# Modulation weights laid out by output, and 24 more gathered rows multiplied during routing

## The chip, the cores and the metric

The kernel runs on one core of one Trainium2 chip. The metric is the device time of one execution in microseconds (us), the median of repeated runs.

## What is computed

The model is a two-layer decoder trunk over 512 tokens of width 1024. Each layer is a mixer (RWKV-7 time mixing beside a pooling mixer) and then an expert feed-forward part (PEER). Both are preceded by RMSNorm and by a modulation: a shift, a scale and a gate for every channel, all computed from one conditioning vector `c`. The reference, cut to what this case touches:

```python
c_act = silu(c)                                   # (1, 1024)
for l in range(2):
    mod = c_act @ ada_w[l] + ada_b[l]             # (1, 6 * 1024)
    sh1, sc1, g1, sh2, sc2, g2 = split(mod, 6)
    h = rmsnorm(x, ln1_g[l]) * (1 + sc1) + sh1
    x = x + g1 * mixer(h)
    h2 = rmsnorm(x, ln2_g[l]) * (1 + sc2) + sh2
    x = x + g2 * peer(h2)

def peer(h):
    q = h @ peer_q                                # 8 heads, 2 halves of 128
    s, i = top_k(q . keys, 16)                    # per token, head and half
    top_s, sel = top_k(s0 + s1, 16)               # 16 of 256 pairs per token and head
    idx, gate = pairs[sel], softmax(top_s)        # 128 experts per token
    act = gelu(h . u[idx])                        # u, v: 16384 rows of 1024
    return sum(gate * act * v[idx])
```

## The kernel before

TensorE (PE) multiplies 128x128 blocks. The weights in fp32 are split into a high and a low part by ScalarE (ACT, line 281) and VectorE (DVE, line 282), and each product takes three matmuls of the parts (`mm3`, line 299). `split_next` loads a weight tile into one of three `raw` buffers and splits it into one of three `wsp` buffers, so the split runs at most three tiles ahead of PE.

The 512 tokens of a layer's PEER part are treated in two ways. For the last 384 tokens ("dense"), all 16384 experts are computed in 128 chunks of 128 experts: `s_chunk` multiplies the tokens with a chunk of `u` (24 matmuls of 384 columns), then gelu, then a multiplication by a gate table, then `back` multiplies with the chunk of `v` (18 matmuls of 512 columns, line 1193). For the first 128 tokens ("gathered"), only the 128 chosen experts per token are read: one indirect DMA on the GpSimd queue (POOL, line 884) fetches one row of `u` or of `v` for each of the 128 tokens, a tile of 128x1024 fp32. There are 128 tiles of `u` and 128 of `v` in each layer. DVE multiplies each `u` tile with the tokens and sums along the row (line 890, with a second instruction that reads the sum), and each `v` tile is added into the output with its weight (line 898).

The stages of a layer, in the order of the program, are these.

1. The mixer, lines 340 to 840. At its start in layer 0 four groups of modulation values are computed (`ada_both`, lines 204 to 220) before the first projection can run; six more groups in each layer's mixer (`ADA_MIX`) are computed beside the mixer's work (`ada_step`, line 782).
2. The query stage, lines 1080 to 1095: 16 query projections, each followed by scores and by four top-16 selections on DVE. Beside it, six more groups of modulation values in layer 0 and two in layer 1 (`ADA_PRE`).
3. Routing. For each of the four token tiles DVE picks the 16 best pairs of each head (`pick`). POOL multiplies the masks (line 1002), DVE sums them (line 988). For the three dense tiles it then builds one-hot tables (lines 1055 to 1058), which PE turns into the gate table (line 1075). The picks of the third and fourth tile run interleaved with the first 32 of 48 one-hot blocks; the last 16 blocks run without picks. Beside all routing, the first `SPILL` = 88 chunks of `u` are multiplied (`s_ahead`) and their gelu is written to memory. In the part with one-hot blocks, the first `GPRE` = 24 gathered tiles are loaded and multiplied (`gather_step`), three buffers at a time.
4. The dense stage, the loop of lines 1237 to 1247: `front`, `values`, `gathers` and `back` for each chunk. Chunks 0 to 87 read their gelu back; chunks 88 to 127 compute it. The function `upto` says how many gathered tiles are loaded by chunk c: 0.9 per chunk up to chunk 87, then the rest evenly until `GEND` = 4 chunks before the end. With 24 + 79 tiles done by chunk 87, 153 are left for 36 chunks, 4.25 for each.
5. The ends: the last three chunks are multiplied tile by tile, and `finish` and `update` treat each token tile, the gathered one (number 0) first.

Each modulation group is 512 outputs. Its weights lie by input: a tile holds 128 inputs x 512 outputs. DVE multiplies eight such half tiles with a per-partition scalar and adds them up (line 195 for the first, line 197 for the other seven). Four matmuls with a column of ones (line 227) then sum over the partitions. Each of these is two weight loads and two passes on PE, eight in all for a group. At the start of layer 0, `ada_both` gives half of the eight tiles directly to PE (line 213). Each engine runs its instructions in a fixed order; a scheduler sets it when the program is built, from the order of the code, the buffers, and its own estimate of when things are ready.

## Time and profile before

| what | value |
|---|---|
| median of 3 runs | 3393.1 us (3392.6 to 3399.39) |
| profiled execution: its own time | 3396.74 us |
| profiled execution: span of the trace | 3395.0 us |
| PE busy (weight loads beside it) | 3211.9 us, 95% (2810.6 us, 83%) |
| DVE busy | 2713.8 us, 80% |
| ACT, POOL busy | 1397.3 us, 41%; 828.7 us, 24% |
| mean granted PE clock | 0.957 of full speed |
| moved by DMA | 826.48 MB, mean 243 GB/s |

The span runs from the first to the last instruction; the 1.7 us between it and the execution's own time lie around the trace. Busy shares are means over stages with different limits, so each stage is read by itself, in windows of time.

### The profile page before, as it was taken

The numbers are of one execution on the slowest core, as the hardware profiler recorded it, in microseconds if no ns is written. First come the engines' busy times: TensorE is split into PE (matmuls) and PEld (weight loads), VectorE is DVE, ScalarE is ACT, GpSimd is POOL, SyncE is SP. The second block draws the span as 40 slices with busy tenths as digits, with TensorE's granted clock in tenths as the row PEclk, the third lists the DMA queues.
The fourth block names the chain that finished last, engine by engine and source line by source line (L and its number), as shares of the span: only waits on it lengthen the run. The fifth ranks groups of instructions, "written<-read, shape, count | busy, mean of one in ns | idle before, by whom it ended". The sixth has DMA issues, their size and how long they took to land. (4 is left out here: it accounts for less than half of the span.)

```text
span 3395.0 us, 52138 instructions
## 1 busy us (share of the span) xinstructions
PE 3211.9 (95%) x18762; PEld 2810.6 (83%) x18762; DVE 2713.8 (80%) x6065; ACT 1397.3 (41%) x2281; POOL 828.7 (24%) x675
## 2 busy tenths in 40 slices
PE   7999889999999999999999999999999999999997
PEld 5787678989998888888777877899999788888886
DVE  4577599888868888899938766988887688888888
ACT  2543223455653334333353523334556433333333
POOL 0000001232202222655500000032230222255554
PEclk8988899999999999999999989999999999999998
DMA  5224353577799999999922234256778999999996
GB/s 192 69 69 151 109 164 118 175 238 255 258 324 346 343 347 337 353 396 383 361 79 86 83 106 155 77 161 195 261 250 291 329 341 340 341 351 335 356 353 260
DMA packets 361380, 826.48 MB, mean 243 GB/s; under 512 B 46496, under 2 KB 189600, under 8 KB 357792
## 3 DMA queue, kind: packets, MB, share of 16 engines
q1 hardware_dynamic: 287392, 554.68, 48.7%
q0 software_dynamic: 73728, 268.47, 21.0%
q8 instruction: 147, 2.41, 0.3%
q14 instruction: 113, 0.93, 0.1%
HBM read 730.75 MB, written 92.27 MB: 242 GB/s over the span
## 5 line engine op out<-in xcount | busy, mean ns | idle before, releaser
L1193 PE MATMUL ps<-vv,wg 128*128 128x512 f32 x4608 | 1081.0, 393 | 23.0 <-ACT vv L1176 11.9
L299 PE MATMUL pss<-hi,wsp 128*128 128x384 f32 (+1 forms) x4880 | 1002.2, 356 | 66.4 <-DVE wsp L282 28.2
L1193 PEld LDWEIGHTS ps<-vv,wg 128*128 128x128 f32 x4608 | 869.1, 189 | 209.1 <-ACT vv L1176 17.5
L299 PEld LDWEIGHTS pss<-hi,wsp 128*128 128x128 f32 x4880 | 879.2, 193 | 126.5 <-DVE wsp L282 38.3
L281 ACT ACTIVATE wsp<-raw 128x1024 fp32r<-128x1024 f32 x341 | 359.6, 1056 | 517.4 <-PE pss L299 352.3
L884 POOL DMA_INDIRECT row<-u,ex x256 | 319.6, 1249 | 845.7 <-DVE row L890 649.6
L299 PE MATMUL pss<-lo,wsp 128*128 128x384 f32 (+1 forms) x2440 | 501.6, 346 | 0.0
L282 DVE TENSOR_TENSOR wsp<-raw,wsp 128x1024 fp32r<-128x1024 f32 x341 | 426.0, 1250 | 66.8 <-ACT wsp L281 65.4
L299 PEld LDWEIGHTS pss<-lo,wsp 128*128 128x128 f32 x2440 | 436.5, 189 | 17.4 <-issue 0.8
L884 POOL DMA_INDIRECT row<-v,ex x256 | 336.8, 1316 | 244.3 <-DVE ox L898 196.1
L1177 DVE TENSOR_TENSOR vv<-raw,vv 128x512 fp32r<-128x512 f32 x512 | 344.4, 690 | 41.7 <-ACT vv L1176 41.6
L1176 ACT ACTIVATE vv<-raw 128x512 fp32r<-128x512 f32 x512 | 291.2, 618 | 110.6 <-DMA raw<-v 74.8
L1167 ACT ACTIVATE wg<-ge 128x384 fp32r<-128x384 f32 x256 | 133.0, 524 | 492.3 <-DVE ge L1165 198.3
L890 DVE SCALAR_TENSOR_TENSOR row<-row,hx 128x1024 f32<-128x1024 f32 x256 | 310.8, 1219 | 24.5 <-DMA row<-u,ex 24.4
L898 DVE SCALAR_TENSOR_TENSOR ox<-row,wx,ox 128x1024 f32<-128x1024 f32 x254 | 325.3, 1281 | 2.3
L1002 POOL TENSOR_TENSOR eq<-same,cid 128x400 f32<-128x400 f16 x128 | 146.8, 1167 | 502.3 <-DVE same L998 307.2
L966 POOL TENSOR_TENSOR hf<-hi,lo 128x128 f32<-128x128 f32 x16 | 8.1, 524 | 933.8 <-DVE tw L935 877.6
L1168 DVE TENSOR_TENSOR wg<-ge,wg 128x384 fp32r<-128x384 f32 x256 | 141.4, 555 | 104.4 <-ACT wg L1167 99.8
L1077 ACT ACTIVATE gb<-ps 128x512 f32<-128x512 f32 x192 | 200.1, 1163 | 0.0
L1165 DVE TENSOR_TENSOR ge<-ge,g 128x192 f32<-128x192 f32 x496 | 157.0, 353 | 49.9 <-DMA g<-gscr 32.2
L1160 ACT ACTIVATE ge<-pss 128x384 f32<-128x384 f32 x80 | 39.2, 490 | 264.6 <-PE pss L299 264.4
L1075 PE MATMUL ps<-oh,oh 128*128 128x128 f16 x1536 | 105.4, 220 | 0.0
(461 smaller groups left out, 3258.1 us busy)
## 6 DMA issues: line engine op xcount, KB each, us to landing
raw<-uT SPq DMA_DIRECT2D x256, 512.0 KB, 4.9
raw<-v SPq DMA_DIRECT2D x256, 512.0 KB, 6.6
gscr<-gb SPq DMA_DIRECT2D x24, 2048.0 KB, 8.2
g<-gscr SPq DMA_DIRECT2D x124, 384.0 KB, 7.5
gespill<-ge SPq DMA_DIRECT2D x176, 192.0 KB, 4.1
ge<-gespill SPq DMA_DIRECT2D x176, 192.0 KB, 6.2
ada<-ada SPq DMA_DIRECT2D x96, 256.0 KB, 5.4
raw<-ada SPq DMA_DIRECT2D x48, 512.0 KB, 3.7
```

What stands on the lines that cost most here:

```text
L281: S.activation(w[:, 0], raw, AF.Copy)
L282: V.tensor_tensor(w[:, 1], raw, w[:, 0].bitcast(F32), op=ALU.subtract)
L299: TE.matmul(pt, w[:, a, k * P:(k + 1) * P], hs[k][b], start=start and n == 0, stop=stop and n == len(steps) - 1)
L884: G.indirect_dma_start(out=rows[n], out_offset=None, in_=A["u" if n < P else "v"], in_offset=bass.IndirectOffsetOnAxis(ap=ex[:, n % P:n % ...
L890: V.scalar_tensor_tensor(row, row, 1.0, hx, op0=ALU.mult, op1=ALU.mult, accum_out=dots[:, e:e + 1])
L898: V.scalar_tensor_tensor(ox, row, wx[:, e:e + 1], ox, op0=ALU.mult, op1=ALU.add)
L1002: pace["G"] = G.tensor_tensor(eq, same[:, q // 2:q // 2 + 4], z["id"][:, h].unsqueeze(1).unsqueeze(3).to_broadcast([P, 4, NC, 2]), op=ALU. ...
L1077: S.activation(gb[:, :, o:o + 4].rearrange("p i t -> p t i"), pt, AF.Copy, scale=1.0 / GSC)
L1165: V.tensor_tensor(gq, gq, g[:, :, c % IG], op=ALU.mult)
L1176: S.activation(vv[0][q], raw[:, q * T:(q + 1) * T], AF.Copy)
L1177: vlo[q] = V.tensor_tensor(vv[1][q], raw[:, q * T:(q + 1) * T], vv[0][q].bitcast(F32), op=ALU.subtract)
L1193: end[0] = TE.matmul(acc[t][d2], wg[a][:, ts_], vv[b][d2], start=(c == 0 and a == 0 and b == 0), stop=(c == NK - 1 and a == 1))
```

## The change

Three things change.

- **Modulation weights by output.** The weights are stored transposed: a tile holds 128 outputs x 1024 inputs. The activated vector `silu(c)` is held in all 128 partitions (a 512 KB load at the start in place of 4 KB). DVE multiplies a tile with it and sums along the row in one instruction with an accumulator output, four tiles for a group, and the sums land where the modulation values belong. The eight PE passes of each group go (and the 32 + 8 of `ada_both` groups at the start). At the start of layer 0 the tiles come in two halves of 512 inputs, eight instructions for a group. The tiles of the query stage now use the gather buffers (`row`, three of them) in place of small tiles.
- **`GPRE` 24 to 48.** 24 more tiles of `u` are loaded and multiplied during routing. By chunk 87, 48 + 79 = 127 tiles are done in place of 103.
- **`GEND` 4 to 8.** The remaining 129 tiles are spread over 32 chunks, 4.03 for each, and the last eight chunks have none.

The small-tile pool shrinks from 38 to 36 tiles (`S2`) to make room for the vector.

```diff
--- before
+++ after
-GPRE = 24
+GPRE = 48
-GEND = 4
+GEND = 8
-S2 = 38
+S2 = 36
...
-    ct = pers.tile([P, ND], F32, name="ct")
-    nc.sync.dma_start(ct, A["cT"])
-    sc_ = pers.tile([P, ND], F32, name="silu_c")
-    S.activation(sc_, ct, AF.Sigmoid)
-    V.tensor_tensor(sc_, sc_, ct, op=ALU.mult)
+    silu = pers.tile([P, D], F32, name="silu")
+    for q in range(2):
+        nc.sync.dma_start(silu[:, q * T:(q + 1) * T], A["cB"][:, q * T:(q + 1) * T])
+        sg = s2t("sg")
+        S.activation(sg, silu[:, q * T:(q + 1) * T], AF.Sigmoid)
+        V.tensor_tensor(silu[:, q * T:(q + 1) * T], silu[:, q * T:(q + 1) * T], sg, op=ALU.mult)
...
-    def ada_acc(l, g, side=0, early=False):
...
-    def ada_both(l, g):
...
-    def ada_mod(l, g, acc):
-        pt = acc
-        if acc.shape[-1] > 4:
-            pt = sbank((P, 4))
-            for m in range(4):
-                TE.matmul(pt[:, m:m + 1], acc[:, m * P:(m + 1) * P], C("one"), start=True, stop=True)
+    def ada_rows(l, g, where="raw"):
+        dst = mods[l][:, 4 * g:4 * g + 4]
+        more = s2t("half", (P, 4)) if where == "half" else None
+        for m in range(4):
+            if where == "half":
+                for q, out in enumerate((dst, more)):
+                    w = s2t("ada")
+                    first["dma"] = nc.sync.dma_start(w, A["adaT"][l, g, m, :, q * T:(q + 1) * T])
+                    V.scalar_tensor_tensor(w, w, 1.0, silu[:, q * T:(q + 1) * T], op0=ALU.mult, op1=ALU.mult, accum_out=out[:, m:m + 1])
+            else:
+                w = st.tile([P, D], F32, tag="raw", name=nm("raw")) if where == "raw" else rpool[0].tile([P, D], F32, tag="row", name=nm("row"), bufs=rpool[1])
+                nc.sync.dma_start(w, A["adaT"][l, g, m])
+                V.scalar_tensor_tensor(w, w, 1.0, silu, op0=ALU.mult, op1=ALU.mult, accum_out=dst[:, m:m + 1])
+        return more
+
+    def ada_mod(l, g, more=None):
+        dst = mods[l][:, 4 * g:4 * g + 4]
+        if more is not None:
+            V.tensor_tensor(dst, dst, more, op=ALU.add)
         o = VOFF["adab"][0]
-        V.tensor_tensor(mods[l][:, 4 * g:4 * g + 4], pt, vecs[l][:, o + 4 * g:o + 4 * g + 4], op=ALU.add)
+        V.tensor_tensor(dst, dst, vecs[l][:, o + 4 * g:o + 4 * g + 4], op=ALU.add)
...
-                accs = {2: ada_both(0, 2)}
+                accs = {2: ada_rows(0, 2, "half")}
...
-                        accs[i] = ada_acc(*todo[i])
+                        accs[i] = ada_rows(*todo[i])
...
-                            adas.append((hp, *pre[0], ada_acc(*pre.pop(0), early=True)))
+                            adas.append((hp, *pre[0], ada_rows(*pre.pop(0), "row")))
...
-    a["cT"] = cols(f("c")[0])
+    a["cB"] = np.broadcast_to(f("c")[0], (P, D))
-    a["ada"] = f("ada_w").reshape(L, 4, 2, P, 12, T).transpose(0, 4, 1, 3, 2, 5)
+    a["adaT"] = f("ada_w").transpose(0, 2, 1).reshape(L, 12, 4, P, D)
```

The scheduler's order moves with it. Three places follow, all on DVE. The numbers behind names only tell buffers apart. Line 890 becomes 859, line 282 becomes 251, line 998 becomes 967, line 988 becomes 957, lines 1055 to 1058 become 1024 to 1027, line 898 becomes 867.

The first place is the end of the mixer of layer 0: the last of eight updates of `x` (line 823, now 792), the reciprocal root of the norm (line 840, now 809), and the first normalised tile (line 328, now 297), on which all query projections wait. Before:

```order
L823 SCALAR_TENSOR_TENSOR x_3235<-pss_3242,mod_105,x_3235 128x512
L282 TENSOR_TENSOR wsp_3275<-raw_3273,wsp_3275 128x1024
L830 TENSOR_TENSOR sq_3107<-sq_3107,sq_3268 128x512
L924 CAST iot<-const 128x256
L823 SCALAR_TENSOR_TENSOR x_3271<-ps_3278,mod_105,x_3271 128x512
L282 TENSOR_TENSOR wsp_3415<-raw_3413,wsp_3415 128x1024
L838 TENSOR_TENSOR rs<-pss_3306,rs 128x4
L840 RECIPROCAL rs<-rs 128x4
L328 SCALAR_TENSOR_TENSOR nt_3333<-x_3101,A_0_109,ps_3328 128x512
```

Now:

```order
L799 TENSOR_TENSOR sq_2987<-sq_2987,sq_3148 128x512
L893 CAST iot<-const 128x256
L189 SCALAR_TENSOR_TENSOR row_3356,mod_109<-row_3356,silu 128x1024
L792 SCALAR_TENSOR_TENSOR x_3151<-ps_3158,mod_109,x_3151 128x512
L189 SCALAR_TENSOR_TENSOR row_3359,mod_109<-row_3359,silu 128x1024
L251 TENSOR_TENSOR wsp_3295<-raw_3293,wsp_3295 128x1024
L189 SCALAR_TENSOR_TENSOR row_3362,mod_109<-row_3362,silu 128x1024
L807 TENSOR_TENSOR rs<-pss_3186,rs 128x4
L809 RECIPROCAL rs<-rs 128x4
L189 SCALAR_TENSOR_TENSOR row_3365,mod_109<-row_3365,silu 128x1024
L197 TENSOR_TENSOR mod_109<-mod_109,vec_87 128x4
L189 SCALAR_TENSOR_TENSOR row_3504,mod_109<-row_3504,silu 128x1024
L297 SCALAR_TENSOR_TENSOR nt_3213<-x_2981,A_0_113,ps_3208 128x512
```

Five modulation tiles (`row<-row,silu`) stand ahead of the first normalised tile, where none stood. Of the 24 such tiles of layer 0's query stage, 12 stand ahead of the first top-16 selection (of 48 half-size instructions, 3 stood there before). In layer 1 five stand ahead of the first normalised tile too, and all eight ahead of the first selection.

The second place is one pick with its one-hot block in routing, layer 0. `same` is the comparison that POOL waits for, `eq` what POOL gives back, `oh` the one-hot tables, `wsp` the split that PE waits for, `row` a gathered tile. Before:

```order
L1058 TENSOR_TENSOR oh_5798<-iot,selj 128x1024
L282 TENSOR_TENSOR wsp_6423<-raw_6421,wsp_6423 128x1024
L1055 TENSOR_TENSOR oh_5799<-iot,seli 128x1024
L998 TENSOR_TENSOR same_6466<-iot,r_5808 128x800
L282 TENSOR_TENSOR wsp_6474<-raw_6472,wsp_6474 128x1024
L988 TENSOR_REDUCE r_5808<-eq_6468 128x8
L988 TENSOR_REDUCE r_5808<-eq_6470 128x8
L935 MATCH_REPLACE tw_6564<-r_5808,cv_5806 128x50
```

Now:

```order
L251 TENSOR_TENSOR wsp_6207<-raw_6205,wsp_6207 128x1024
L967 TENSOR_TENSOR same_6250<-iot,r_5580 128x800
L859 SCALAR_TENSOR_TENSOR row_6130,dots<-row_6130,hx 128x1024
L1024 TENSOR_TENSOR oh_5571<-iot,seli 128x1024
L859 SCALAR_TENSOR_TENSOR row_6238,dots<-row_6238,hx 128x1024
L957 TENSOR_REDUCE r_5580<-eq_6252 128x8
L251 TENSOR_TENSOR wsp_6258<-raw_6256,wsp_6258 128x1024
L957 TENSOR_REDUCE r_5580<-eq_6254 128x8
L904 MATCH_REPLACE tw_6354<-r_5580,cv_5578 128x50
L859 SCALAR_TENSOR_TENSOR row_6289,dots<-row_6289,hx 128x1024
```

Three gathered tiles stand where none stood. From the first one-hot block to the last selection of the fourth tile, 17 gathered tiles stood and now 34 do, among 32 one-hot blocks in both; the splits (line 282) there go from 47 to 46. Layer 1 has the same counts.

The third place is the end of the dense stage of layer 1: `ox` is the gathered output, `vv` and `wg` are what the last chunks' matmuls wait for, `o` is the finish of the gathered tile. Before:

```order
L898 SCALAR_TENSOR_TENSOR ox<-row_30197,wx,ox 128x1024
L898 SCALAR_TENSOR_TENSOR ox<-row_30266,wx,ox 128x1024
L1177 TENSOR_TENSOR vv_24668<-raw_30394,vv_24666 128x512
L1177 TENSOR_TENSOR vv_24669<-raw_30394,vv_24667 128x512
L898 SCALAR_TENSOR_TENSOR ox<-row_30268,wx,ox 128x1024
L1165 TENSOR_TENSOR ge_24267<-ge_24267,g_30227 128x192
L1165 TENSOR_TENSOR ge_24267<-ge_24267,g_30229 128x192
L898 SCALAR_TENSOR_TENSOR ox<-row_30270,wx,ox 128x1024
L1168 TENSOR_TENSOR wg_24663<-ge_24267,wg_24662 128x384
L898 SCALAR_TENSOR_TENSOR ox<-row_30272,wx,ox 128x1024
L1177 TENSOR_TENSOR vv_24672<-raw_30430,vv_24670 128x512
L1177 TENSOR_TENSOR vv_24673<-raw_30430,vv_24671 128x512
```

Now:

```order
L1130 TENSOR_TENSOR ge_24009<-ge_24009,g_29665 128x192
L867 SCALAR_TENSOR_TENSOR ox<-row_29708,wx,ox 128x1024
L1133 TENSOR_TENSOR wg_24415<-ge_24009,wg_24414 128x384
L251 TENSOR_TENSOR wsp_29743<-raw_29741,wsp_29743 128x1024
L867 SCALAR_TENSOR_TENSOR ox<-row_29710,wx,ox 128x1024
L1142 TENSOR_TENSOR vv_24422<-raw_29794,vv_24420 128x512
L1192 TENSOR_TENSOR o_30114<-ox,rowb_25602 128x512
L1142 TENSOR_TENSOR vv_24423<-raw_29794,vv_24421 128x512
L251 TENSOR_TENSOR wsp_29802<-raw_29800,wsp_29802 128x1024
L1142 TENSOR_TENSOR vv_24426<-raw_29853,vv_24424 128x512
L1142 TENSOR_TENSOR vv_24427<-raw_29853,vv_24425 128x512
L1192 TENSOR_TENSOR o_30115<-ox,rowb_25741 128x512
```

Before, gathered tiles stand between the last `vv` and `wg` up to the very last one. Now the last gathered tile has five chunks' `wg` behind it (six in layer 0), and the finish of the gathered tile stands among them.

## Rows read from the trace of the kernel before

**Rows 1.** Time windows, stage by stage: length, busy us (instructions) per engine, granted clock, DMA share, GB/s

```profile
400.00:450.00 50.00, 44.37 (x205) 36.43 (x204) 36.01 (x99) 17.14 (x27) 0.00 (x0) 0.93 0.50 159
500.00:550.00 50.00, 45.54 (x243) 39.27 (x242) 50.00 (x253) 14.20 (x21) 0.00 (x0) 0.97 0.43 138
655.00:760.00 105.00, 95.67 (x639) 92.67 (x639) 91.15 (x209) 50.75 (x63) 32.24 (x25) 0.98 0.66 214
760.00:785.00 25.00, 25.00 (x198) 24.36 (x197) 20.08 (x34) 17.17 (x20) 1.80 (x2) 1.00 0.80 280
785.00:890.00 105.00, 102.52 (x707) 100.25 (x706) 93.18 (x212) 55.53 (x68) 34.15 (x25) 0.98 0.75 255
890.00:985.00 95.00, 95.00 (x761) 92.17 (x759) 73.94 (x105) 66.94 (x79) 6.18 (x4) 1.00 0.78 280
1460.00:1500.00 40.00, 40.00 (x204) 36.01 (x203) 39.80 (x48) 14.20 (x24) 23.33 (x19) 1.00 1.03 400
3213.00:3253.00 40.00, 35.92 (x177) 31.38 (x176) 35.89 (x45) 13.76 (x23) 23.27 (x18) 1.00 0.97 352
```

**Rows 2.** Groups of instructions, shapes kept apart: count | busy us, mean ns of one | idle before them

```profile
L197 DVE SCALAR_TENSOR_TENSOR acc<-raw,silu_c,acc 128x512 f32<-128x512 f32 x84 | 62.4, 743 | 2.4 <-DMA raw<-ada 1.9
L195 DVE TENSOR_SCALAR acc<-raw,silu_c 128x512 f32<-128x512 f32 x12 | 5.8, 481 | 2.3 <-DMA raw<-ada 2.3
L227 PEld LDWEIGHTS pss<-const,acc 128*128 128x128 f32 x160 | 21.9, 203 | 5.0 <-issue 1.6 <-DVE x L823 1.5 <-DVE acc L197 0.5
L890 DVE SCALAR_TENSOR_TENSOR row<-row,hx 128x1024 f32<-128x1024 f32 x256 | 310.8, 1219 | 24.5 <-DMA row<-u,ex 24.4
L890 DVE DVE_READ_ACCUMULATOR row<-row,hx 128x1 f32 x256 | 21.1, 82 | 0.0
```

**Rows 3.** Timeline of the start: start us, us, engine, line, what [idle before]

```profile
31.51 3.35 DVE L321 RECIPROCAL rs<-rs 128x512 f32<-128x512 f32 x1 [3.90 <-ACT rs L320]
65.21 5.56 PE L299 MATMUL ps<-hi,wsp 128*128 128x512 f32 x14 [1.01 <-ACT hi L330]
```

**Rows 4.** Line L945, the end of each query projection, layer 0 and layer 1

```profile
L945 ACT ACTIVATE qT<-pss x16: 578/594/599, 429.9 to 544.8; 128x512 f32<-128x512 f32 x16
L945 ACT ACTIVATE qT<-pss x16: 578/597/600, 2096.1 to 2194.3; 128x512 f32<-128x512 f32 x16
```

**Rows 5.** What VectorE waited for from 655 to 890 us: us in total, times, longest

```profile
DVE row L890 <- DMA row<-u,ex: 10.9, 3, 4.3
DVE r L988 <- POOL eq L1002: 7.5, 12, 1.3
```

**Rows 6.** Timeline of ScalarE: the gelu that ends a dense chunk, layer 0, then layer 1

```profile
1368.37 0.49 ACT L1160 ACTIVATE ge<-pss 128x384 f32<-128x384 f32 x1 [9.29 <-PE pss L299]
1680.68 0.49 ACT L1160 ACTIVATE ge<-pss 128x384 f32<-128x384 f32 x1 [4.59 <-PE pss L299]
...
3013.28 0.49 ACT L1160 ACTIVATE ge<-pss 128x384 f32<-128x384 f32 x1 [3.56 <-PE pss L299]
3021.58 0.49 ACT L1160 ACTIVATE ge<-pss 128x384 f32<-128x384 f32 x1 [5.32 <-PE pss L299]
...
3361.62 0.49 ACT L1160 ACTIVATE ge<-pss 128x384 f32<-128x384 f32 x1 [3.01 <-PE pss L299]
```

**Rows 7.** Timeline at the end of the dense stage of layer 0

```profile
1683.97 1.31 PE L1193 MATMUL ps<-vv,wg 128*128 128x512 f32 x2 [1.93 <-ACT vv L1176]
...
1687.83 2.07 PE L1193 MATMUL ps<-vv,wg 128*128 128x512 f32 x4 [2.54 <-DVE vv L1177]
...
1696.91 5.98 PE L1193 MATMUL ps<-vv,wg 128*128 128x512 f32 x18 [2.05 <-DVE wsp L282]
```

**Rows 8.** Timeline at the end of the program

```profile
3378.09 1.28 DVE L1227 TENSOR_TENSOR o<-ps,rowb 128x512 f32<-128x512 f32 x2
...
3390.23 1.42 DVE L1234 SCALAR_TENSOR_TENSOR o<-o,ss,rowb 128x512 f32<-128x512 f32 x2
```

**Rows 9.** Line L282 on VectorE from 655 to 890 us: duration in ns min/median/max, first and last start

```profile
L282 DVE TENSOR_TENSOR wsp<-raw,wsp x46: 1204/1220/1922, 657.1 to 885.9; 128x1024 fp32r<-128x1024 f32 x46
```

More of the change, by code (lines that the diff above doesn't have):

```diff
@@ L262, in body @@
     rs = pers.tile([P, 2, NT], F32, name="rs")
+    rpool = [None, 0]
     normed, seq = [], []
@@ L349, in mixer @@
             if l == 0:
-                accs = {2: ada_both(0, 2)}
+                accs = {2: ada_rows(0, 2, "half")}
                 rstd = rms_rstd()
                 for i, g in enumerate((2, 0, 3, 1)):
-                    ada_mod(0, g, accs.pop(g) if g in accs else ada_both(0, g))
+                    ada_mod(0, g, accs.pop(g) if g in accs else ada_rows(0, g, "half"))
                     if i == 1:
@@ L879, in peer @@
             pace, adas = {}, []
-            rows, rpool = {}, [None, 0]
+            rows = {}
             def gather_load(n):
```

45 lines of the change are left out of this document (removed).

## The prediction

> **What bounds the kernel now.** The table of busy times gives PE 95%, but the change leaves nearly all of PE's work alone, so I read windows of single stages first [rows 1], then what ends the idle time in each. In the query stage DVE is the bound: 36.01 of 50 us busy while the top-16 selections have not begun, 50.00 of 50 later, with PE at 45.54. In the stretch of picks and one-hot blocks, 655 to 890 us, DVE has 91.15 + 20.08 + 93.18 = 204.4 us of work in 235 us and PE 95.67 + 25.00 + 102.52 = 223.2. The remaining 31 us of DVE are waits and hand-overs; those for gathered rows sum to 10.9 us in 3 waits, those for POOL's `eq` to 7.5 us in 12 [rows 5]. From 890 to 985 us PE is full (95.00 of 95) and DVE has 21 us to spare. In the late dense stage of layer 0 PE is full and DVE nearly so (39.80 of 40); in layer 1 PE has 35.92 of 40 while the DMA engines are busy throughout (0.97). So DVE's own order, and the arrival of rows, decide most of what this change touches.
>
> **The change, part by part.** The sum is made against the profiled execution, 3396.74 us; the median of 3393.1 lies 3.6 us lower, and the end is moved by that. About 0.2%, or 6.8 us, is what a measurement of this kernel can tell from no change.
>
> *Start.* The reciprocal root of the first norm starts at 31.51 us and the second half of the first projection at 65.21 [rows 3]. The squares' matmuls no longer stand on PE between matmuls that wait for modulation weights, but DVE gets four more 512-wide multiplies per group; one costs about 0.743 + 0.082 = 0.82 us with the reading of its sum [rows 2], 13 us over four groups, most of which I put into the time in which the weights are still on their way. I take -4. Bounds: +2, if part of the 13 us shows, and -8.
>
> *Mixers.* A group loses eight passes on PE: the 160 loads of line 227 are 20 groups, 21.9 / 20 = 1.1 us each [rows 2]. Six groups in each mixer give 6.6 us a layer if PE was full there, nothing if the passes filled gaps. I take half, -3 a layer, -6 together, within [-13, 0]. On DVE a group goes from 0.481 + 7 x 0.743 = 5.68 us to an estimated 4 x (1.219 + 0.082) = 5.20, so nothing new arises there.
>
> *Query stage.* It runs 114.9 us in layer 0 with six groups and 98.2 in layer 1 with two [rows 4]: 16.7 / 4 = 4.2 us per group, near the 5.68 that a group costs a full DVE. By the order, 12 of the 24 tiles in layer 0 now come ahead of the first selection, 12 x 1.3 = 15.6 us in the time when DVE has 14 of 50 us idle; before, 3 of 48 half tiles did. Five of them stand ahead of the first normalised tile, on which all projections wait. Since only three row buffers feed them, that can delay PE by 2 to 4 us. I take -8 in layer 0 and -3 in layer 1, -11 together. Bounds: -22, if groups cost the stage nothing and PE waits for none, and +4, if the saving is nil and PE waits.
>
> *Picks.* The stretch gets 34 gathered tiles in place of 17: 17 x 1.30 = +22.1 us of DVE. One split fewer takes 1.2 off [rows 9], and leaves one chunk's 24 matmuls for the stretch where PE is full: half of an undisturbed chunk's 8.30 us [rows 6], since 24 matmuls of 384 columns are as many columns as the 18 of 512 that make up the other half, so +4.2 us. DVE then needs 204.4 + 22.1 - 1.2 = 225.3. The waits for `eq` fall from 7.5 to about 3, because rows now stand between `same` and `eq`. With w for row waits the layer moves by 225.3 + 3 + w + 4.2 - 235, about w - 3. Before, 3 rows of 17 waited 3.6 us each; rows now load twice as often through the same three buffers, but DVE also has more work to do between arrivals. I take w = 12 in each layer, near the measured 10.9, so +9 each, +18 together. Bounds: 0, if DVE's slack takes all, and +36, at w = 21, twice the measured. The other 7 rows fall into the last 16 one-hot blocks and cost at most 9.1 us of the 21 that DVE has spare there; were that cover gone, 9.1 is their price.
>
> *Late dense stage.* In layer 1, 39 periods of gelu take 3361.62 - 3013.28 = 348.3 us [rows 6]. The first, undisturbed one is 8.30, which makes 39 x 8.31 = 324.1 and 24.2 us of stall. A chunk reads, by shapes, 0.52 MB each of `u` and `v`, 0.1 of gates and 4.25 rows of 0.52, about 3.37 MB; now it is 4.03 rows, 3.26 MB, 3.4% less. 348.3 - 3 x 8.31 is 323 for 36 chunks, 9.0 each; 3.4% of that is 0.3, times 31 chunks 9.5. The four more chunks without rows go from 9.0 to 8.31, 2.8. Together -12, within [-24, -3]. In layer 0, 37 periods take 312.3, only 4.8 above 37 x 8.31; I take -2, within [-4.8, 0]. Early in the dense stage PE is full and the pace of rows is unchanged: nothing.
>
> *Ends.* In layer 0 PE waits 1.93 + 2.54 + 2.05 = 6.5 us at the last chunks, for `vv` and a split that stand behind DVE's rows [rows 7]. With the last row five or six chunks back I take these and a little of the gathered tile's earlier update: -8, within [-10, -4]. In layer 1 the last finishes of the dense tiles stand behind tile 0's, the final one starting at 3390.23 [rows 8]; tile 0's now goes ahead of the last chunks. -7, within [-10, -3].
>
> Sum: -4 - 6 - 11 + 18 - 14 - 15 = -32. That is 3364.7 on the profiled execution's scale, **3361 us** as a median (0.9% faster).
>
> **A rule beside the row on transfers.** Layer 1's late chunks move 352 GB/s at a DMA share of 0.97, layer 0's 400 at 1.03 [rows 1]: the same demand, 12% apart, with the queues full in both. The Trainium skill, HBM, section "Specifications (TRN2)", says that a core streaming alone gets about 425 GB/s, bounded by its 16 DMA engines; by that, an estimated 3.37 MB / 8.31 us = 405 GB/s fits, layer 1's stall is not one of bytes, and fewer bytes would give about -2 there. The trace disagrees with that ceiling for gathered rows, since 352 is all that layer 1 gets with the engines full.
>
> **Rivals.**
>
> *All rows hide in the picks.* The 18 us fall away and the sum is -50: 3343. For it: 31 us of DVE idle stand against 22 of new work. Against: the measured waits for rows.
>
> *Slower: rows come late in the picks.* The place is line 890 between `same` and the one-hot tables. Three buffers, with loads issued twice as often, can leave many tiles unarrived when DVE reaches them, and everything behind stands: `wsp` for PE, `same` for POOL. If 12 of 34 wait 3.2 us, w = 38 and a layer costs +35. In place of 18 that is 70: -50 + 70 = +20, 3413. The change breaks even at w = 28 a layer, some 9 waits. For it: three such waits already at half the rate, up to 4.3 us [rows 5]. Against: over half of DVE's work lies between two uses, time for a load.
>
> *Layer 1's dense stall is latency, not bytes.* Then the late stage gives -2 in place of -14: 3373. For it: 400 GB/s were moved in layer 0.
>
> *The new layout does nothing.* PE's passes filled gaps, and DVE trades like for like: start, mixers and query stage at 0 give -11, 3382. For it: 5.68 against 5.20 us a group; against it, the idle DVE early in the query stage.
>
> *VectorE and GpSimd block each other.* The splits reach 1922 ns against a median of 1220 [rows 9], while POOL multiplies masks in the same stretch. If each of 17 more two-input tiles paid 0.7 us, that is 12 us a layer: -32 + 24 = -8, 3385. The Trainium skill, SBUF — State Buffer, section "Who interferes with whom", says that a DVE instruction with two SBUF inputs contends with a GpSimd instruction that reads SBUF, and that the one that comes second fully blocks. By that rule every tile that meets a mask product pays; the trace bears it out only in part, since the splits' median stands 16 ns above their minimum of 1204.
>
> **How the numbers follow.** The forecast has 0.36; its own range is 3350 to 3373. All rows hidden 0.13, rows late 0.17, latency 0.13, layout nothing 0.15, blocking 0.06. The range must leave out no more than 0.2: from 3338, a little below the first rival, to 3398, which takes in the three middle ones and the milder part of late rows (w up to 30); beyond it lie most of that case and the tails of the forecast. Faster by over 0.2% (below 3386): the forecast, hidden rows, latency, and most of the layout and blocking cases, 0.71. Within 0.2%: what remains of these and the mild late rows, 0.13. Slower: most of late rows with a part of the mishaps around the start and the first normalised tile, 0.16.
>
> **What would show it.** In the profile after: the reciprocal near 28 us and the second half near 61; the query projections spanning about 107 and 95 us; in the pick stretch DVE at some 225 us busy, waits for rows about 12 us and for `eq` about 3 in a layer; 39 gelu periods near 336 us in layer 1; none of the three waits at the end of layer 0; the last instruction of line 1234 starting within some 5 us of PE's end. I am wrong if row waits in the pick stretch exceed 28 us a layer, if the projections span as long as before, or if layer 1's late periods stay at 9.0 us with fewer rows.

## The result, and the profile after

| | before | changed |
|---|---|---|
| median | 3394.78 us (3392.6 to 3399.39, 4 runs) | 3424.79 us (3414.13 to 3436.51, 4 runs) |
| ratio | 1 | 1.0074, 95% interval 1.0047 to 1.0100 |
| profiled execution, span | 3396.74, 3395.0 us | 3414.13, 3412.3 us |

The change makes the kernel 0.5 to 1.0% slower. The forecast was 3361, range 3338 to 3398. The profiled execution is the shortest of the four changed ones, so the spans show 17.3 of some 30 us. The table cuts them at single rows; each line is the length of a stage after less its length before, beside the forecast's term.

| stage, from row to row | forecast | measured |
|---|---|---|
| start, to the second half of the first projection (65.21, now 50.80) | -4 | -14.4 |
| mixer of layer 0, to the reciprocal ahead of the query stage (413.5, now 404.5) | -3 | +5.4 |
| query stage, to the last projection (544.8, now 522.3) | -8 | -13.5 |
| routing, to the last one-hot matmul (985.8, now 995.8) | +9 | +32.5 |
| early dense stage, to the first late gelu (1340.17, now 1349.45) | 0 | -0.7 |
| late dense stage, to the last gelu (1680.68, now 1701.74) | -2 | +11.8 |
| end of layer 0, to the reciprocal (1718.3, now 1727.5) | -8 | -11.9 |
| mixer of layer 1 (2079.7, now 2104.2) | -3 | +15.3 |
| query stage (2194.3, now 2212.8) | -3 | -6.0 |
| routing (2634.1, now 2681.3) | +9 | +28.7 |
| early dense stage (3013.28, now 3060.46) | 0 | 0.0 |
| late dense stage (3361.62, now 3389.41) | -12 | -19.4 |
| end of the program | -7 | -10.5 |

The rows of the changed kernel that answer to [rows 3], [rows 6] and [rows 8], from its timeline, and then those that answer to [rows 4], from its line of query projections:

```profile
19.52 3.34 DVE L290 RECIPROCAL rs<-rs 128x512 f32<-128x512 f32 x1
50.80 5.17 PE L268 MATMUL ps<-hi,wsp 128*128 128x512 f32 x14 [9.71 <-ACT hi L299]
...
1701.74 0.49 ACT L1125 ACTIVATE ge<-pss 128x384 f32<-128x384 f32 x1 [2.31 <-PE pss L268]
3060.46 0.49 ACT L1125 ACTIVATE ge<-pss 128x384 f32<-128x384 f32 x1 [3.67 <-PE pss L268]
3389.41 0.49 ACT L1125 ACTIVATE ge<-pss 128x384 f32<-128x384 f32 x1 [2.39 <-PE pss L268]
3407.66 1.42 DVE L1199 SCALAR_TENSOR_TENSOR o<-o,ss,rowb 128x512 f32<-128x512 f32 x2
```

```profile
L914 ACT ACTIVATE qT<-pss x16: 578/597/600, 422.5 to 522.3; 128x512 f32<-128x512 f32 x16
L914 ACT ACTIVATE qT<-pss x16: 579/597/599, 2122.0 to 2212.8; 128x512 f32<-128x512 f32 x16
```

The first norm is 12 us earlier: the squares' 16 matmuls now run together from 7.89 us on, where they stood between modulation matmuls from 16.73 to 30.75 before. The projections take 99.9 and 90.8 us.

Routing is where the time goes. Windows over the picks and over the last blocks, then two stretches inside the picks (columns as in [rows 1]):

```profile
635.00:900.00 265.00, 231.93 (x1539) 223.43 (x1538) 219.94 (x489) 121.98 (x152) 90.25 (x67) 0.94 0.71 243
900.00:995.00 95.00, 95.00 (x760) 92.17 (x758) 81.52 (x119) 67.20 (x79) 17.40 (x11) 1.00 0.89 321
817.00:827.00 10.00, 0.02 (x1) 0.00 (x0) 3.36 (x7) 3.67 (x5) 0.00 (x0) 0.60 0.70 274
827.00:836.00 9.00, 7.34 (x33) 7.08 (x34) 8.38 (x16) 2.65 (x4) 7.07 (x3) 0.50 0.73 291
```

The first took 235 us before, the second 95 as now [rows 1]. DVE's work rose from 204.4 to 219.9 us, less than the 225.3 that were worked out; its waits rose too. What DVE waited for there, in layer 0 and then in layer 1 (us in total, times, longest; before: [rows 5]):

```profile
DVE row L859 <- DMA row<-u,ex: 27.8, 14, 6.6
DVE r L957 <- POOL eq L971: 6.9, 12, 0.8
...
DVE row L859 <- DMA row<-u,ex: 31.0, 15, 5.9
DVE r L957 <- POOL eq L971: 6.9, 12, 0.8
```

Fourteen rows come late where three did. The longest wait, in the timelines of POOL, DVE and PE:

```profile
809.28 3.61 POOL L971 TENSOR_TENSOR eq<-same,cid 128x400 f32<-128x400 f16 x2 [5.46 <-DVE same L967]
813.03 0.97 POOL L853 DMA_INDIRECT row<-u,ex  x1
828.79 6.36 POOL L971 TENSOR_TENSOR eq<-same,cid 128x400 f32<-128x400 f16 x2 [13.17 <-DVE same L967]
835.29 1.25 POOL L853 DMA_INDIRECT row<-u,ex  x1
...
798.78 0.08 DVE L859 DVE_READ_ACCUMULATOR row<-row,hx 128x1 f32 x1
823.97 1.23 DVE L859 SCALAR_TENSOR_TENSOR row<-row,hx 128x1024 f32<-128x1024 f32 x1 [6.64 <-DMA row<-u,ex]
...
804.93 2.94 PE L268 MATMUL pss<-hi,wsp 128*128 128x384 f32 x16
827.14 1.89 PE L1044 MATMUL ps<-oh,oh 128*128 128x128 f16 x16 [10.12 <-DVE oh L1027]
830.54 5.49 PE L268 MATMUL pss<-hi,wsp 128*128 128x384 f32 x16 [1.52 <-ACT ge L840]
```

The buffer is free at 798.86, when DVE has read the sum of the row three back. Its next load stands on POOL behind two mask products, which wait for `same` from DVE; so it is issued at 813.03, 14 us later, and DVE, which reaches the row at 817.3, waits until 823.97. The transfer has its part in this: it took 10.9 us, where the median in the picks is 5.8. Behind the row on DVE stand one-hot tables, for which PE waits 10.12 us. After that PE is slower: 16 matmuls take 5.49 us that took 2.94. The granted clock of 827 to 836 us is 0.50, the level of 1.2 GHz, after 10 us in which PE had nothing to do; the last blocks have 1.00, that of 2.4 GHz.

Late issue is not new. From a buffer's release to its next load 16.8 us passed in the median before (0.3 to 30.3, picks of layer 0) and 9.0 now (0.3 to 27.9). What changed is when DVE comes back to that buffer: 37 us after the release before, 18.5 now, again medians.

### The profile page after: what moved, and what is told of

It is laid out like the page before. It is cut to its first block, busy times and chain, and to the rows that moved or that the text cites. A ratio compares the mean times of both kernels' runs of the same rounds, so it can differ in the third digit from the quotient of the medians.

```text
span 3412.3 us, 51425 instructions
## 1 busy us (share of the span) xinstructions
PE 3160.5 (93%) x18442; PEld 2770.5 (81%) x18442; DVE 2715.7 (80%) x6118; ACT 1397.7 (41%) x2284; POOL 827.6 (24%) x675
## 5 line engine op out<-in xcount | busy, mean ns | idle before, releaser
L1158 PE MATMUL ps<-vv,wg 128*128 128x512 f32 x4608 | 1069.2, 391 | 12.7 <-ACT vv L1141 7.3
L853 POOL DMA_INDIRECT row<-u,ex x256 | 311.5, 1217 | 775.9 <-DVE row L859 590.0
L1046 ACT ACTIVATE gb<-ps 128x512 f32<-128x512 f32 x192 | 196.9, 1151 | 14.4 <-PE ps L1044 14.4
L1044 PE MATMUL ps<-oh,oh 128*128 128x128 f16 x1536 | 106.5, 222 | 19.6 <-DVE oh L1027 19.6
```

What stands on the lines that cost most here:

```text
L853: G.indirect_dma_start(out=rows[n], out_offset=None, in_=A["u" if n < P else "v"], in_offset=bass.IndirectOffsetOnAxis(ap=ex[:, n % P:n % ...
L1046: S.activation(gb[:, :, o:o + 4].rearrange("p i t -> p t i"), pt, AF.Copy, scale=1.0 / GSC)
L1158: end[0] = TE.matmul(acc[t][d2], wg[a][:, ts_], vv[b][d2], start=(c == 0 and a == 0 and b == 0), stop=(c == NK - 1 and a == 1))
```

## The experiments

**Table of the runs.** Routing runs from the first one-hot table on DVE to the last one-hot matmul on PE, row waits are those of line 890 or its like in that time, the mixers run from the second half of the first projection, or from the reciprocal that ends layer 0, to the reciprocal ahead of the query stage; all in us, from one profile each. Ratios are to the kernel before on the same chip.

| run | ratio, interval | routing L0, L1 | row waits | mixers L0, L1 |
|---|---|---|---|---|
| before | 1 | 334.8, 335.4 | 10.9, 11.5 | 348.3, 361.4 |
| changed | 1.0074, 1.0047 to 1.0100 | 364.9, 366.6 | 27.8, 31.0 | 353.7, 376.7 |
| e1 48 rows alone | 1.0102, 1.0061 to 1.0142 | 367.2, 365.7 | 31.5, 29.9 | |
| e2 layout alone | 0.9959, 0.9934 to 0.9984 | 335.2, 334.5 | 11.3, 12.0 | 355.6, 369.8 |
| e3 early end alone | 1.0009, 0.9982 to 1.0035 | 334.6, 334.8 | 12.3, 10.9 | |
| e4 four buffers | 0.9987, 0.9967 to 1.0008 | 347.7, 350.8 | 14.6, 15.7 | 358.4, 373.2 |
| e5 rows not read | 0.9856, 0.9823 to 0.9888 | 337.0, 337.1 | 0, 0 | 356.1, 375.2 |
| e6 layout, held | 0.9994, 0.9973 to 1.0015 | 333.1, 333.4 | 10.7, 9.5 | 363.5, 380.7 |
| e7 e4 held | 1.0017, 1.0000 to 1.0034 | 347.6, 349.7 | 14.4, 15.6 | 362.6, 379.9 |
| e8 e7, 36 rows | 0.9996, 0.9980 to 1.0013 | 349.6, 346.5 | 21.4, 18.2 | 363.2, 386.9 |
| e9 loads free | 1.0011, 0.9985 to 1.0037 | 356.2, 354.3 | 7.0, 7.1 | |
| e10 e4, loads free | 1.0007, 0.9982 to 1.0031 | 354.6, 353.3 | 9.8, 9.7 | |
| e11 no mixer groups | 0.9826, 0.9768 to 0.9884 | 332.2, 334.1 | 9.8, 10.1 | 329.4, 355.6 |
| e12 plain loads | 0.9986, 0.9964 to 1.0007 | 351.8, 352.7 | 4.1, 4.9 | |
| e13 36 rows, late | 0.9800, 0.9773 to 0.9828 | 322.5, 322.5 | 0.8, 0.7 | 356.9, 368.8 |
| e14 42 rows, late | 0.9851, 0.9809 to 0.9893 | 322.4, 321.1 | 0.5, 1.2 | 357.2, 372.1 |
| e15 layout, halves | 0.9947, 0.9926 to 0.9969 | 332.0, 333.5 | 9.5, 9.6 | 356.2, 374.2 |
| e16 layout, own buffers | 0.9922, 0.9894 to 0.9950 | 331.5, 333.4 | 9.2, 9.4 | 340.9, 369.7 |
| e17 e13 + e16 | 0.9753, 0.9731 to 0.9774 | 322.5, 321.0 | 2.4, 0.9 | 342.3, 373.1 |
| e18 e17, 32 rows | 0.9743, 0.9715 to 0.9771 | 322.4, 322.4 | 1.0, 1.0 | 342.2, 370.0 |

**The parts alone.** e1 and e3 set one constant of the kernel before, e2 sets two of the changed one back.

```diff
-GPRE = 24
+GPRE = 48
```

> The kernel before with 48 rows multiplied in routing and nothing else changed. Theory (the 24 added rows are late, because their loads stand on POOL behind the mask products, and stop DVE and then PE): the stretch of picks loses about 30 us in each layer as in the changed kernel, with waits for rows of 25 to 30 us a layer; the late dense stage of layer 1 gives back 15 to 25; about +35 us in all, 3430. Rival (the loss in the picks comes with the new layout, for instance with what it leaves in the queues): the picks lose under 10 us a layer, and the kernel is 5 to 20 us faster than before.

```diff
-GPRE = 48
-GEND = 8
+GPRE = 24
+GEND = 4
```

> The layout by output alone, with 24 rows and 4 chunks as before. Theory (the layout costs only in the mixers): start -15, mixer of layer 0 +6, query stage -11, mixer of layer 1 +13, query stage of layer 1 -9, picks and dense stage unchanged within 3: about -16 us, 3378. Rival (the layout disturbs the picks too): these lose 10 us or more a layer and the kernel is no faster than before.

```diff
-GEND = 4
+GEND = 8
```

> The kernel before with the gathers ending eight chunks from the end and nothing else changed: 153 rows in 32 chunks, 4.78 for each in place of 4.25. Theory (layer 1's late dense stage is bound by bytes): these chunks read 8% more, about 0.7 us each, +22 us over 32 chunks, less 8 to 15 us at the two ends and in the four chunks more without rows: +5 us, within -5 and +12. Rival (the stall is latency, not bytes): the late periods stay at 9.0 us and only the ends move, -12 to -18 us.

e1 has the whole loss in routing, e2 none of it: the 48 rows are the cause, and the layout is worth 0.2 to 0.7% by itself, less than forecast. e3 changes nothing that can be told from none, but its theory missed in the parts: the late dense stage of layer 1 took 336.0 us, 12.3 less than before with as many rows, where some 22 more were forecast. At its end of layer 1 the last row is loaded 4.9 us before the last gelu and used 5.3 us after it: at 4.78 rows a chunk the rows fall behind, and the eight free chunks are used up by the lag. So the gain at the ends, 11.9 and 10.5 us in the changed kernel, is not that of the earlier end alone: with 48 rows alone layer 1's end already took 23.5 us in place of 33.4, and layer 0's 33.1 in place of 37.7.

**What makes the rows cost.** e4, e5 and e9 change the changed kernel; e10 is e4 with e9's edit.

```diff
-                rpool[:] = rt, 3
+                rpool[:] = rt, 4
...
-                if n > 1:
+                if n > 2:
...
-                        gather_use(n - 2)
+                        gather_use(n - 3)
...
-                gs = [lambda n=n: gather_step(n) for n in range(GPRE + 2)] if GPRE else []
+                gs = [lambda n=n: gather_step(n) for n in range(GPRE + 3)] if GPRE else []
```

> The changed kernel with four row buffers in routing in place of three, and each row used three steps after its load in place of two. Theory (rows late behind POOL's mask products): waits for rows in the stretch of picks fall from 28 us to under 10 in each layer, PE's 10 us wait for one-hot tables goes with them, and each layer wins 15 to 25 us: 3375 to 3395. Rival (DVE's work, or the order with one-hot blocks bunched, is what costs): the waits for rows fall, but the stretch is as long as in the changed kernel within 5 us, 3415 to 3430.

```diff
-                    V.scalar_tensor_tensor(row, row, 1.0, hx, op0=ALU.mult, op1=ALU.mult, accum_out=dots[:, e:e + 1])
+                    if n < GPRE:
+                        V.scalar_tensor_tensor(scr[0], hx, 1.0, hx, op0=ALU.mult, op1=ALU.mult, accum_out=dots[:, e:e + 1])
+                    else:
+                        V.scalar_tensor_tensor(row, row, 1.0, hx, op0=ALU.mult, op1=ALU.mult, accum_out=dots[:, e:e + 1])
...
+                scr[0] = rt.tile([P, D], F32, name="scr")
```

> The changed kernel, but the 48 multiplications of rows in routing take the tokens twice in place of the loaded row, and write to a buffer of their own; the rows are still loaded, and nothing waits for them. It leaves out the reading of those rows. Theory (the waits for rows are what costs in the picks, with PE's waits and the lower clock that follow): the stretch of picks moves by 0 to +6 us in each layer against the kernel before, where the changed kernel has +30: 3365 to 3380 in all. Rival (DVE's 22 us of added work, or the order with the one-hot blocks bunched, costs by itself): the stretch keeps +12 us or more in each layer.

```diff
-                    with tc.issue_after(pace["G"].ins):
-                        gather_load(n)
+                    gather_load(n)
```

> The changed kernel with three row buffers, but a row's load is no longer held behind POOL's latest mask product; it stands on POOL wherever the scheduler puts it. Theory (a load comes late because it stands behind products that wait for DVE): where loads move ahead of products, the time from a buffer's release to the issue of its next load falls from 10 to 28 us, waits for rows fall under 20 us a layer, and the picks lose 5 to 20 us a layer in place of 30. Rival (the transfers themselves, 5 to 11 us each, are the limit with three buffers; or products now wait behind loads): picks +25 us or more a layer.

> Four row buffers, use three steps after the load, and loads not held behind POOL's products. Theory: the two remedies add up, waits for rows under 8 us a layer, picks +2 to +8 a layer in place of +14 with four buffers alone, 3375 to 3388. Rival (the rest of the loss with four buffers is not late rows): picks stay at +12 or more.

```diff
+                if n < GPRE:
+                    nc.sync.dma_start(rows[n], A["u"][l * NK * NK + n * P:l * NK * NK + (n + 1) * P])
+                    return
```

> The changed kernel, but the 48 rows of routing are loaded by plain transfers of as many bytes on SP's queue in place of gathers on POOL's; it leaves out the choice of the rows there. Theory (POOL's order makes the loads late): a load is issued soon after its buffer is free, waits for rows fall under 12 us a layer and the picks lose 2 to 10 us a layer in place of 30. Rival (three buffers or the bytes are the limit, whichever queue): waits stay over 20 us and the picks at +20 or more.

With the same multiplications and no wait for rows (e5) routing takes 337 us, 2 more than before. So DVE's added work fits by itself, and what costs is the tie between loads and multiplications. e5 cuts it both ways: DVE waits for no row, and no load waits for DVE to free a buffer. Four buffers halve the waits and the loss (e4). The windows over the picks, e5 and then e4, and e4's waits there:

```profile
635.00:872.00 237.00, 223.16 (x1531) 217.60 (x1530) 221.66 (x495) 121.94 (x151) 88.18 (x68) 0.98 0.78 269
```

```profile
634.00:882.00 248.00, 227.58 (x1536) 219.66 (x1535) 225.25 (x498) 122.08 (x152) 89.97 (x68) 0.97 0.76 259
```

```profile
DVE row L859 <- DMA row<-u,ex: 14.6, 8, 4.2
DVE r L957 <- POOL eq L971: 4.8, 11, 0.8
```

DVE has 221.7 of 237 us of work in e5: the added rows took most of its slack, and then a wait lengthens the stretch.

e9, e10 and e12 got loads issued sooner (e9 0.3 us after the release in the median), and waits for rows fell to 4 to 10 us, near what the theories had; but routing still takes 17 to 21 us more than before, which those of e10 and e12 had not. e10's rival came true: the rest of the loss is not late rows alone. The waits moved. In e9 POOL stands at loads that wait for a buffer, ahead of mask products; in e12 SP does, ahead of the loads of `u` for the chunks:

```profile
POOL row L853 <- DVE row L859: 73.5, 14, 14.6
```

```profile
SPq L854 <- DVE row L862: 51.2, 24, 6.8
SPq L248 <- DVE wsp L251: 36.9, 23, 4.4
```

SP waited longer for `wsp` in the changed kernel (119.1 us), so its sum alone says little. That these account for the 17 to 21 us was not shown; the cause of this part of the loss stays open between the waits of the loads and what they hold up.

**The mixers.** e6 and e15 change the layout alone, e16 too, with the groups of the mixers loaded as those at the start, in halves into small tiles; e11 leaves the groups out.

```diff
-                            V.tensor_tensor(z[n, h], pts[h], C(mk) ...
+                            vbeat[0] = V.tensor_tensor(z[n, h], pts[h], C(mk) ...
...
-                    with tc.issue_after(beat[0].ins):
+                    with tc.issue_after(vbeat[0].ins):
                         accs[i] = ada_rows(*todo[i])
```

> The layout alone (24 rows, 4 chunks), with the modulation tiles of the mixers held on DVE behind the latest masked product of the recurrence, where they stood before. Theory (the loss in the mixers is the bunching of 24 tiles of 1.3 us ahead of what the recurrence waits for): the mixers go from +4 and +8 with the layout alone to -3 or lower each, so 8 to 20 us under the layout alone: 3365 to 3375. Rival (the mixers lose for another reason, such as the weights' loads or the split buffers that the tiles take): the mixers stay within 3 us of the layout alone, 3385.

```diff
-                        accs[i] = ada_rows(*todo[i])
+                        accs[i] = None
+                        V.tensor_copy(mods[todo[i][0]][:, 4 * todo[i][1]:4 * todo[i][1] + 4], vecs[todo[i][0]][:, VOFF["adab"][0]:VOFF["adab"][0] + 4])
```

> The layout alone (24 rows, 4 chunks) with the loads and multiplications of the twelve modulation groups in the two mixers left out; these groups take the bias alone. It shows what the mixers take without that work. Theory (with the layout, whole tiles of 1.3 us stand in the way of the recurrence's short steps, and cost more than the half tiles and PE passes of before): each mixer is 10 to 20 us shorter than with the layout alone, and 5 to 12 us shorter than before, so that the work of before cost 5 to 12 us and that of now 10 to 20. Rival (the mixers changed for another reason, by where other loads and splits went): without the work they are within 4 us of the layout alone.

```diff
-        more = s2t("half", (P, 4)) if where == "half" else None
+        more = s2t("half", (P, 4)) if where in ("half", "raw") else None
...
-                V.scalar_tensor_tensor(w, w, 1.0, silu, op0=ALU.mult, op1=ALU.mult, accum_out=dst[:, m:m + 1])
+                if where == "raw":
+                    for q, out in enumerate((dst, more)):
+                        wq, sq = w[:, q * T:(q + 1) * T], silu[:, q * T:(q + 1) * T]
+                        V.scalar_tensor_tensor(wq, wq, 1.0, sq, op0=ALU.mult, op1=ALU.mult, accum_out=out[:, m:m + 1])
...
```

> The layout alone, with each modulation tile of the mixers multiplied in two halves of 512 (two instructions of about 0.8 us in place of one of 1.3). Theory (the longer instruction, in the way of the recurrence's short steps, is why the mixers lose): the mixers come back to the kernel before, from +4 and +8 to -2 to +3 each, 3372 to 3382. Rival (the place of the tiles in DVE's order, or the load buffers that they share with the weights): no shorter than the layout alone, or longer by the 7 us of added work a layer.

```diff
-                        accs[i] = ada_rows(*todo[i])
+                        accs[i] = ada_rows(*todo[i], "half")
```

> The layout alone, with the mixers' modulation tiles loaded in halves into small buffers of their own in place of the three that weights are loaded into. Theory (the shared load buffers delay the splits of the output weights, and so PE): the mixers gain 5 to 15 us each against the run with halves in the shared buffers. Rival (DVE's order alone matters): within 3 us of that run.

Where the mixers lose can be read from what PE waits for in mixer 0, in the changed kernel and then before:

```profile
PE ps L597 <- DVE bk L584: 7.1, 1, 7.1
PE pss L630 <- DVE ak L623: 5.3, 1, 5.3
PE ps L639 <- DVE rt L687: 3.0, 1, 3.0
```

```profile
PE pss L661 <- DVE ak L654: 1.7, 1, 1.7
PE ps L628 <- DVE bk L615: 0.4, 1, 0.4
```

`bk`, `ak` and `rt` prepare the recurrence. The 24 modulation tiles stand on DVE from 181 to 242 us, among these steps, where the half tiles of before stood from 250 to 335. PE's work in the mixer fell by 15.9 us, its waits rose by 19.6. e2 has much the same waits.

So the bunching that e6 named is there; its remedy missed. With the tiles held back the mixers are longer still, 363.5 and 380.7. In its mixer 0 the waits for `bk` and `rt` are gone, but the tiles now stand among the steps of the recurrence's state `M`, for which PE's steps wait:

```profile
PE psc L704 <- DVE M L706: 21.7, 15, 3.6
```

Before, the same wait was 2.9 us in the like stretch. Halving the instruction did not help (e15). By e11 the groups cost mixer 0 18.9 us before (348.3 - 329.4) and 26.2 with the layout. Own buffers take 15.3 off the run with halves in mixer 0. SP's queue shows one thing that changed. Loads in e15 and then in e16 (start us, time from first issue to last, what, count):

```profile
168.82 0.33 SPq L253 DMA_DIRECT2D raw<-w_out  x1
175.23 11.37 SPq L188 DMA_DIRECT2D raw<-adaT  x3
...
235.77 42.24 SPq L188 DMA_DIRECT2D raw<-adaT  x13
278.30 0.33 SPq L253 DMA_DIRECT2D raw<-w_out  x1
278.91 38.78 SPq L188 DMA_DIRECT2D raw<-adaT  x8
317.98 4.62 SPq L253 DMA_DIRECT2D raw<-w_out  x3
```

```profile
169.31 17.12 SPq L248 DMA_DIRECT2D raw<-w_out  x4
...
191.03 0.33 SPq L248 DMA_DIRECT2D raw<-w_out  x1
...
214.81 84.23 SPq L184 DMA_DIRECT2D ada<-adaT  x48
```

In shared buffers the modulation tiles stand ahead of the output weights, of which one is loaded at 278 and three from 318 on; with buffers of their own these are there by 192. That this is the cause was not shown, and two runs speak against it as the whole. In e2 the last three output weights are loaded from 236 us on, and its mixer 0 is as long as e15's; before, they came from 332 on, and it was shorter. In e16 DVE also reaches the first modulation tile only at 233 us (179 in e15), PE's waits are 29.4 us in place of 36.6, and the granted clock of the mixer is higher (0.906 and 0.885). In mixer 1 the two runs differ by 4.5 us; the kernel before's own mixer 1 took 361.4, 365.8 and 366.8 us in the profiles of before, e1 and e3, so nothing is settled there.

**Versions.** e7 joins e4 and e6, e8 is e7 with 36 rows. e13 and e14 change the changed kernel so that 17 rows are spread over the blocks with picks and the rest over the last 16 blocks; e17 and e18 add e16's edit, with 36 and 32 rows.

> The changed kernel with both repairs: modulation tiles held in the mixers, and four row buffers with use three steps after the load. Theory (mixers and rows add up): the 3395 of four buffers less 10 to 20 us, 3375 to 3387. Rival (the repairs overlap, or the holding only moves the wait to the query stage): 3390 to 3400.

> The same as the kernel with both repairs, with 36 rows in routing in place of 48. Theory (the loss in the picks grows with how often loads are issued behind POOL's products, and is small at 36 rows with four buffers): picks +3 to +8 us a layer in place of +14, the late dense stage of each layer 3 to 6 us longer than with 48 rows: 3365 to 3378, under both neighbours (24 and 48 rows). Rival (every row in the picks costs its 1.3 us): between them in proportion, no better than 24 rows.

```diff
-GPRE = 48
+GPRE = 36
...
                 for t in range(1, NT):
+                    if t == NT - 1:
+                        cut3 = len(main)
...
-                cuts = [0, len(steps0), len(steps0 + steps1), len(main)]
+                cuts = [0, len(steps0), len(steps0 + steps1), cut3, len(main)]
...
-                    blend(main[cuts[i]:cuts[i + 1]], sl[at[i]:at[i + 1]], ([], gs[:g1], gs[g1:])[i])
+                    blend(main[cuts[i]:cuts[i + 1]], sl[at[i]:at[i + 1]], ([], [], gs[:17], gs[17:])[i])
```

> The changed kernel with 36 rows in routing: 17 spread over the one-hot blocks that run with picks, as before, and 19 over the last 16 blocks, where DVE has time to spare. Theory (what costs is more rows where DVE is already full, each wait there adding to the stretch): the picks move by under 4 us a layer and the last blocks by under 4, while the ends and the late dense stage keep 15 to 30 us of the gain: 3350 to 3372, faster than the kernel before, the changed kernel and the layout alone. Rival (any row more in routing costs its 1.3 us, wherever it stands): picks and last blocks together lose 12 us or more a layer.

> The same with 42 rows, 17 with the picks and 25 in the last 16 blocks. Theory: these need 82 us of DVE's other work and 25 x 1.3 = 33 of 119 us; they still fit, last blocks +0 to +5 us a layer, and the late dense stage gains some 2 to 4 us a layer more than with 36: 3345 to 3370. Rival (PE begins to wait for splits and one-hot tables there): last blocks +8 us or more a layer, and no faster than 36 rows.

> 36 rows, 17 of them with the picks and the rest over the last blocks, and the mixers' modulation tiles in halves in buffers of their own. Theory (the two gains are in different stages and add up): the 3334 of 36 rows less 14 to 22 us, 3312 to 3322. Rival (the own buffers only moved a wait that the later stages give back): 3328 to 3336.

> The same with 32 rows. With 36, 32 rows were multiplied by the end of the one-hot blocks and four after them, and the first dense chunks came 9 to 10 us later than those blocks' end would have them. Theory (the four left over delay the dense stage's start): that delay falls under 3 us a layer, the late dense stage loses 1 to 3 us a layer, 4 to 16 us under the run with 36 rows. Rival (the delay has another cause, or the late stage needs the four rows more): the same as with 36 rows within 4 us, or slower.

e7 and e8 missed: holding costs, and 36 rows spread evenly over the same blocks still wait 21.4 us. e13 does better than expected, 2.0% under the kernel before. e14 lies in its range at 3350, but by another way than its theory: the rows over 32 did not fit. Windows over the picks and last blocks of e13:

```profile
635.00:844.00 209.00, 206.65 (x1430) 202.66 (x1429) 187.18 (x426) 112.98 (x139) 55.67 (x45) 0.99 0.70 235
844.00:957.00 113.00, 113.00 (x897) 109.73 (x897) 99.05 (x157) 78.36 (x91) 31.13 (x23) 1.00 0.92 347
```

These windows are cut earlier in the work than those of [rows 1]. From the first one-hot table to the last mask sum on DVE e13 takes 212.1 us, the kernel before 220.9 and the changed one 252.1; from there to the last one-hot matmul 110.3, 113.9 and 112.8. The edit also deals out the chunks of `u` anew, but in the first stretch PE runs 1053 of their matmuls in e13 and 1057 before, so the rows are what differs: 13 there and 19 behind in e13, 16 and 8 before, 32 and 16 in the changed kernel. Waits for rows are 0.8 us in place of 10.9, and routing is 12.3 us shorter than before: even the 24 rows of before had a price. Only 32 rows fit. With 36 and 42 the rest delays the first dense chunks of layer 0; from the last one-hot matmul to the first late gelu, e13 takes 364.8 us, e14 374.5, before 354.4. What PE waits for from 940 to 1060 us, e13 and then e18 (32 rows, 354.0 us):

```profile
PE ps L1160 <- ACT vv L1143: 8.2, 3, 6.4
```

```profile
PE ps L1160 <- ACT vv L1143: 1.7, 2, 1.0
```

e17, which differs from e18 in the four rows alone, takes 362.3 us: the delay is that of rows left over. It does not pay in layer 0, where the late dense stage and the end together take 11.2 us more in e18 than in e17. In total the two cannot be told apart; both are about 2.5% under the kernel before.

## Why the prediction was wrong

- **Picks, the step that failed.** "I take w = 12 in each layer, near the measured 10.9". It was 27.8 and 31.0. A second term was put at nothing without a reason: of the 31 us in which DVE stood idle before, 12.2 are neither waits for rows nor for `eq`, and "225.3 + 3 + w + 4.2 - 235" has no place for them; 10.4 of them were still there after. With the measured waits that sum gives 225.3 + 6.9 + 27.8 + 4.2 - 235 = +29 in layer 0, and measured are +30.1 from the first table to the last matmul, but this is luck: DVE's work came out 5.4 us below 225.3, and the 4.2 us of PE did not show, the last blocks taking 95 us as before. What the trace adds up to is +15.5 of work, +16.9 of waits for rows and -2.4 of other idle time. The mechanism is in the main the rival's ("rows come late in the picks"), near its price of +35 and just about its break-even of 28 us, at which the whole sum would give no change; e9, e10 and e12 leave 17 to 21 us of the loss with few such waits, so what the rows do there is not all told by w. The reason that I gave for w, "DVE also has more work to do between arrivals", does not hold: DVE came back to a buffer 18.5 us after its release, where it had been 37, and a load that is issued 9 us after the release and takes 4 to 12 us to land leaves little of that. [rows 5] counted three waits; the time from a buffer's release to its next load and next use, to be read line by line, would have told more.
- **Mixers, wrong in sign.** "On DVE a group goes from [...] 5.68 us to an estimated [...] 5.20, so nothing new arises there." Totals were right; but the tiles moved in DVE's order ahead of `bk`, `ak` and `rt`, and PE waits 15.4 us for these in mixer 0, where it had waited 2.1: more than the 6.6 us of passes saved. -3 each was forecast, +5.4 and +15.3 measured; in mixer 1 a part of the latter is the spread of the kernel before (361.4 to 366.8).
- **Start, right in kind, too small.** -14.4 against -4, outside the bound of -8: the squares stood longer between modulation matmuls than I allowed.
- **Query stage, right in kind, too small.** -13.5 and -6.0 against -8 and -3, within the bounds; the projections take 99.9 and 90.8 us where some 107 and 95 were named. From the reciprocal to the end of the first projection it is 1.6 and 1.4 us longer, where 2 to 4 were feared for the five tiles.
- **Ends, right in kind, too small.** -11.9 and -10.5 against -8 and -7, beyond the bound of -10 in both; no wait of [rows 7] is left at the end of layer 0.
- **Late dense stage, wrong in layer 0.** Layer 1 gave -19.4 (-12 forecast), layer 0 +11.8 (-2). The loss in layer 0 is not the luck of one profile: the six with 24 rows and the old end (before, e2, e6, e11, e15, e16) took 337 to 352 us, 344.0 in the mean, the seven with 48 rows and the new end (changed, e4, e5, e7, e9, e10, e12) 352 to 358, 355.8 in the mean. Its cause stays open. In layer 1 the same means are 344.9 and 329.8, so about -15. Bytes or latency is not settled: fewer rows went with a shorter stage, but e3 took 336.0 us there with as many rows as before. The Trainium skill, HBM, section "Specifications (TRN2)", gives about 425 GB/s for a core alone. No window shown here reaches it, but the changed kernel's layer 1 moved 398 GB/s from 3265 to 3345 us. So the prediction's "352 is all that layer 1 gets" does not hold.
- **Blocking of VectorE and GpSimd** is small on DVE's side: in the window of the picks of layer 0 the 34 multiplications of rows have a median of 1224 ns, as 1220 before, and two took 1834 and 1925. The Trainium skill, SBUF — State Buffer, section "Who interferes with whom", says that issue order decides who blocks. These rows show at most two tiles that waited. On POOL's side two mask products, one in each layer, took 5.5 us, where before none took over 1.9. The one at 828.79 us ran while DVE had eight one-hot instructions in a row, and the load behind it was issued at 835.29, 25 us after its buffer came free.

## What to carry to other kernels

Before adding work to an engine that has slack, count how often it will wait for data while doing it: work that fills the slack turns every wait that was hidden into time. For a load issued on a busy engine's queue, read three times, not one: when its buffer came free, when it was issued, when it landed. And put added work where the bound is another engine: here 16 rows more among the picks cost some 30 us a layer, and 11 more in the last blocks, where PE is full and DVE is not, cost nothing.

## What the runs showed of the hardware

After PE's wait of 10.12 us the granted clock of the next 9 us was 0.50, and 16 matmuls took 5.49 us in place of 2.94: a wait on a bound engine cost more than its length. A mask product on POOL took 5.5 us beside eight one-hot instructions of DVE, where the median in the picks is 1.36. The changed kernel's four executions lie 22 us apart and those of e13 5 us, with the same instructions each time; why was not looked into.
